# Where the partial sums of a seven-product block multiplication are combined, in a fp32 encoder trunk

## The chip, the core and the metric

The kernel runs on one core of one Trainium2 chip. The metric is the device time in microseconds (us) of one execution. TensorE (PE) multiplies matrices into PSUM, which has eight banks of 512 fp32 columns for each of the 128 partitions. ScalarE (ACT) and VectorE (DVE) read and write both PSUM and SBUF, GpSimd (POOL) here does small work and issues the transfers that add to what is in SBUF, and SyncE (SP) issues the plain loads.

## The reference

Two layers, each of them (`x` is 256 tokens by 1024):

```
x = x + 1/2 * SwiGLU_1(RMSNorm(x))      # w_gate, w_up: 1024 x 2816, w_down: 2816 x 1024
h = RMSNorm(x);  qA kA vA qB kB vB = h @ W_in
oA = windowed attention with a sink;  oB = differential attention
x = x + concat(oA, oB) @ W_out
x = x + 1/2 * SwiGLU_2(RMSNorm(x))      # silu(h @ w_gate) * (h @ w_up) @ w_down
```

and a last RMSNorm. All is fp32. There are four SwiGLU blocks (two in each layer); the change is in them.

## The kernel before

**Precision.** Each fp32 operand is split into a high part (a rounded copy, made by ACT, called a cast below) and a low part (the rest, made by a DVE subtraction). A product is then three matmuls: high by high, low by high, high by low. `emit_split` (line 191) splits weights in halves of a step: a step is a 512 x 512 weight block of 1 MB, half of it is 128 x 1024 elements, and its two parts take two of the 28 `s4` tiles.

**A SwiGLU block** (`ffn`, line 602) works through the 2816 columns in five groups of 512 and a rest of 256. A group makes gate and up products for both token halves (t = 0 and 1, 128 tokens each), silu, the product with the gate (`up`), the transposition of that hidden tile (`turn`), and the product with the down weights, whose sums for two halves of the 1024 outputs stay in four PSUM banks (`accs`) through the whole block.

**Seven products.** In a plain group the gate and up products are eight block products (token half by half of the 1024 inputs by gate/up) of 12 matmuls each. In the groups named in `SEVEN` (2, 3 and 4 in the first SwiGLU block, 1 to 4 in the other three, 15 groups in all) `by_seven` (line 637) makes seven, after Strassen and Winograd, out of sums of the operands. The sums on the token side come once per block from `make_sums`. On the weight side a group has the blocks a, b, c, d and uses a, b + c, d, c, a + b, a + b + c and a + b + c + d. Two of those additions are made by transfers that add (`gather`, issued by POOL: a gets b, b gets c), two by DVE (`plus`, line 131, in two instructions each). The seven products are then combined: ACT copies two of them out of PSUM (`m1`, `m7`), and DVE makes five further sums (`put`).

**What sets the order.** The instructions of PE, and here also of ACT, DVE and POOL, are kept in the order in which the program issues them (`Kept`, line 40; every instruction of theirs carries line 50). PE's order is written by hand. Around it, `weights(less, held)` (line 249) takes the next step for PE and first calls `ahead(2 * i + look[0] - less)`: this issues the splits of all half-steps up to that number, with the `prep` of a step (a `plus` or a `gather`) ahead of its splits, and the loads. When PE's third of four k-chunks of a step is issued, `part` calls `ahead` again for one half-step more, unless the step was taken with `held=True`. So `look[0]` is how many half-steps ACT and DVE are to be ahead of PE, and a split that is issued before another ACT or DVE instruction also runs before it. In the seven-product groups `look[0]` is 8, 7, 6, 5 for groups 1 to 4, and 6, 6, 5 for groups 2 to 4 of the first block.

**PSUM.** All PSUM tiles come from one pool of eight banks (`bank`, line 71). A tile gets a bank whose earlier tile has been read for the last time.

Of the kernel before, what the change touches and what calls it, by code (L numbers as in the profile page):

```python
# [9 lines left out]
F32 = mybir.dt.float32  # L10
F32R = mybir.dt.float32r
AF = mybir.ActivationFunctionType
ALU = mybir.AluOpType
# [21 lines left out]
def trunk(ctx: ExitStack, tc: tile.TileContext, x, n1, g1, u1, d1, nm, w_in, sink,  # L35
# [35 lines left out]
    def bank():  # L71
        return ps.tile([P, 512], F32, tag="ps", bufs=8, name=nm_("ps"))

# [18 lines left out]
    class Step:  # L92
        def __init__(self, kn, n, moves, key=None, prep=None, src=None, free=None, behind=None):
            self.kn, self.n, self.moves, self.prep = kn, n, moves, prep
            self.behind = behind
# [132 lines left out]
    def ahead(n):  # L228

        n = min(n, 2 * len(specs) - 1)  # L230
        while True:
            if at["split"] <= n and at["prep"] > at["split"] // 2:
# [26 lines left out]
    for l in range(DEPTH):  # L259
        def ffn_specs(wg, wu, wd, sevens):  # L260
# [3 lines left out]
            for g in range(1, NGRP):  # L264
                downs = [down(g - 1, h) for h in range(2)]
                if g in sevens:
                    specs.extend(seven(wg[l], wu[l], g * 512, downs, g == 1))
                else:
                    specs.extend(plain(w[l], g * 512, 512, k0, 4) for w in (wg, wu) for k0 in (0, 4))
                    specs.extend(downs)  # L270
            for k0 in (0, 4):
# [34 lines left out]
    class Norm:  # L306
# [42 lines left out]
        def make_sums(self):  # L349
# [18 lines left out]

            s1 = add(b1, t1, ALU.subtract)
            s2 = add(s1, t0, ALU.add)  # L370
            yield
            high(s1)
            high(s2)
            yield
            low(0, s1)
            b0_ = add(b0, s2, ALU.subtract)
            low(1, s2)
            v = add(t1, t0, ALU.subtract)
            yield
            high(b0_)  # L380
            high(v)
            yield
            low(2, b0_)
            low(3, v)
            yield
# [144 lines left out]
    def tokens(accs, xs, w, k0, ks=range(4), first=0, last=KC - 1, order=None, cols=slice(None), h=None):  # L530

        for k, t in (order or [(k, t) for k in ks for t in range(2)]):
            kk = k0 + k
            hi, lo = w.part(k, cols, h)
            xv = xs[kk // 2][:, kk % 2]
            xh, xl = xv[:, t * P:(t + 1) * P], xv[:, S + t * P:S + (t + 1) * P]
            pe.matmul(accs[t], lhsT=xh, rhs=hi, start=kk == first, stop=False)
# [22 lines left out]
    def first_groups(norm, ws):  # L560

        sls = [halves(bank()) for _ in ws]
        for k in range(0, KC, 2):
# [38 lines left out]
    def ffn(norm, aside=None, before=None, final=False, sevens=SEVEN[1]):  # L602
# [33 lines left out]

        def by_seven(h, g):


            flat = lambda: tmp().rearrange("p a n -> p (a n)")  # L640

            def put(o, x, y, op):
                dve.tensor_tensor(o, x, y, op=op)
                return o

            late, run = g == max(sevens), 1 in sevens
            m1, m7 = flat(), flat()


            if g > 1:  # L650
                g0 = prod(norm.quarter(0, 0), weights())
                act.copy(m1, g0)
                p7 = prod(norm.summed(3), weights(1, True))
                act.copy(m7, p7)
                hT = turn(h, 2)
                prod(norm.quarter(0, 1), weights(), g0)
                p3 = prod(norm.summed(2), weights())
                if not run:
                    g0 = silu(flat(), g0, 0)
                down(hT, g - 1, 0, weights())  # L660
                if run:
                    g0 = silu(flat(), g0, 0)
            else:
                p1 = prod(norm.quarter(0, 0), weights(1, True))
                hT = turn(h, (0,))
                w = weights(1, True)
                act.copy(m1, p1)
                p2 = prod(norm.quarter(0, 1), w)
                hT += turn(h, (1,))
                g0 = put(flat(), p2, m1, ALU.add)  # L670
                down(hT, 0, 0, weights())
                silu(g0, g0, 0)
                p3 = prod(norm.summed(2), weights())
                p7 = prod(norm.summed(3), weights(1, True))
                act.copy(m7, p7)
            h = blk(F32)
            p5 = prod(norm.summed(0), weights())
            prod(norm.summed(1), weights(look[0] - 5 if late else run, late or run), p7)
            u1 = put(m1, p7, m1, ALU.subtract)
            p4 = prod(norm.quarter(1, 1), weights(look[0] - 4 if late else 3 * run, late or run))  # L680
            g1 = put(flat(), p4, u1, ALU.subtract)
            w = weights(look[0] - 3 if late else 2 * run)
            silu(g1, g1, 1)
            put(u1, u1, p5, ALU.subtract)
            u0 = put(m7, u1, m7, ALU.subtract)
            put(u0, u0, p3, ALU.add)
            if run and g == max(sevens) - 1:
                ahead(2 * at["use"] - 2 + look[0] - 1)
            up(h, u0, g0, 0)
            up(h, u1, g1, 1)  # L690
            down(hT, g - 1, 1, w)
            return h

# [11 lines left out]

        accs = [[bank(), bank()] for _ in range(2)]

        def down(hT, g, h, w):
            tokens(accs[h], [None] * (2 * g) + hT, w, 4 * g, last=(FC - 1, G4 - 1) if final and h else FC - 1)


        gs, us = [bank(), bank()], [bank(), bank()]
        if before is None:
# [33 lines left out]
        for n in range(1, NGRP):  # L747
            if n in sevens:
                look[0] = IN_FFN + min(sevens) - n if before is not take_x else IN_MIX - (n == NGRP - 1)
                h = by_seven(h, n)  # L750
                continue
            sums = norm.make_sums()
            gs = [bank(), bank()]
            tokens(gs, norm.xs, weights(), 0)
            hT = turn(h, 2)
            norm.copies()
# [4 lines left out]
            us = [bank(), bank()]  # L761
# [4 lines left out]
            for hh in range(2):  # L766
                down(hT, n - 1, hh, weights())
                if hh == 0:
                    next(sums, None)

        gu = [bank(), bank()]
        tokens(gu, norm.xs, weights(), 0)
# [55 lines left out]
    def mix(l, norm, nxt_norm):  # L828
# [23 lines left out]

        def scores(q, kb, dist, slopes, init, den):

            sl = [bank(), bank()]
            for t in range(2):
# [19 lines left out]
        def soft_b(h, q):  # L876

            den = den_b[:, h]
            e, _ = scores(q, kbs["b", h], distB, [slopeB[h]] * 2, [3e38] * 4, den)
            d2 = den.rearrange("p (t a) -> p a t", a=2)  # L880
# [56 lines left out]
        vB = tp.tile([P, 2, 512], F32, tag="v", bufs=1, name=nm_("v"))  # L937
        vsl = [bank() for _ in range(2)]
        for k0 in (0, 4):
# [44 lines left out]
        oT = [blk() for _ in range(4)]  # L984
        rsl, osl = [[bank() for _ in range(2)] for _ in range(2)]
        for t in range(2):
# [175 lines left out]
```

## Time and profile before

| | us |
|---|---|
| time, median of 3 runs | 918.64 (917.53 to 919.39) |
| time of the profiled execution | 917.39 |
| its span, first to last instruction | 915.6 |
| TensorE busy (99% of the span) | 904.5 |
| VectorE busy (87%) | 792.5 |
| ScalarE busy (64%) | 589.8 |
| GpSimd busy (7%) | 66.4 |

A row of a timeline has the start, the length, the engine, the source line, the operation, the tile that is written and those that are read (w is a split weight, raw a loaded one, ps a PSUM tile, s an `s4` tile, q and v the token-side sums), and in brackets idle time before it with what ended that. Where several instructions are merged into one row, the length is that of all of them. Matmuls overlap: the time from one start to the next is what one costs PE.

### The profile page before, as it was taken

The page shows a single profiled execution, that of the slowest core. Times are in us where ns is not written, and L with a number is a line of the kernel's source. Part 1 is how long each engine was busy: PE and PEld are TensorE (multiplying, and loading weights), DVE is VectorE, ACT ScalarE, POOL GpSimd, SP SyncE. Part 2 cuts the span into 40 slices and gives each one's busy share as a digit, 9 for nine tenths or more (in the row PEclk, how much of TensorE's full clock was granted, in tenths as well). Part 3 has the DMA queues.
Part 4 walks back from the last instruction along what each step waited for, and adds up shares of the span by engine and source line. Part 5 has one row for each costly group of instructions (what it writes and reads, how often), then busy time and mean ns, then how long its engine had stood idle before and what let it go on. Part 6 is the DMA issues. An engine that isn't in the chain of part 4 may idle for free.

```text
span 915.6 us, 12544 instructions
## 1 busy us (share of the span) xinstructions
PE 904.5 (99%) x4696; PEld 763.7 (83%) x4696; DVE 792.5 (87%) x1096; ACT 589.8 (64%) x917; POOL 66.4 (7%) x83
## 2 busy tenths in 40 slices
PE   8999999999999999999999999999999999999997
PEld 6888888899888888888888888888998888888886
DVE  6768999959975999999789999997797689999994
ACT  7836676557865766576486666665677496666561
POOL 0400100000010100100010010000001010010011
PEclk9999999999999999999999999999999999999999
DMA  9996898828436698898767998887463467998831
GB/s 339 355 238 173 265 297 268 238 93 240 136 108 189 158 280 248 257 273 275 258 164 201 276 285 217 265 293 219 116 230 98 139 153 201 275 289 230 259 132 47
DMA packets 114061, 200.87 MB, mean 219 GB/s; under 512 B 3662, under 2 KB 31376, under 8 KB 114000
## 3 DMA queue, kind: packets, MB, share of 16 engines
q1 hardware_dynamic: 96528, 166.74, 54.5%
q0 software_dynamic: 16096, 31.75, 19.3%
q10 hardware_dynamic: 1376, 1.57, 0.5%
q8 instruction: 37, 0.61, 0.3%
q14 instruction: 24, 0.20, 0.1%
HBM read 199.00 MB, written 1.05 MB: 218 GB/s over the span
## 4 chain that ended last, share of the span: by engine, by line
PE 98%; issue 1%; DMA 0%; ACT 0%; DVE 0%; POOLq 0%; POOL 0%; ACTq 0%
PE ps L50 98%; DMA xk<-in_x_dram 0%; ACT w L50 0%; DVE s L50 0%; DVE xk L50 0%; ACT tmp L50 0%; ACT L50 0%; POOLq L1157 0%; POOL rf L50 0%; ACTq L50 0%; DVE tot L50 0%; DVE tmp L50 0%
## 5 line engine op out<-in xcount | busy, mean ns | idle before, releaser
L50 PE MATMUL ps<-w,s 128*128 128x512 f32 (+1 forms) x2574 | 600.2, 391 | 0.5 <-ACT tmp L50 0.5
L50 PEld LDWEIGHTS ps<-w,s 128*128 128x128 f32 x2574 | 477.6, 188 | 100.3 <-ACT tmp L50 2.3
L50 DVE TENSOR_TENSOR w<-raw,w 128x1024 fp32r<-128x1024 f32 (+1 forms) x458 | 482.1, 1101 | 37.8 <-ACT w L50 36.6
L50 ACT CAST w<-raw 128x1024 fp32r<-128x1024 f32 (+1 forms) x458 | 409.8, 954 | 122.6 <-DVE raw L50 78.4
L50 PE MATMUL ps<-w,q 128*128 128x512 f32 x540 | 127.3, 389 | 0.0
L50 PEld LDWEIGHTS ps<-w,q 128*128 128x128 f32 x540 | 101.4, 188 | 21.0
L50 PE MATMUL ps<-s,w 128*128 128x256 f32 x672 | 83.1, 284 | 0.0
L50 PEld LDWEIGHTS ps<-s,w 128*128 128x128 f32 x672 | 81.5, 192 | 0.5
L50 POOL DMA_DIRECT2D raw<-in_ffn_w_up_dram x30 | 38.9, 1296 | 472.8 <-DVE w L50 240.8
L50 DVE TENSOR_TENSOR raw<-raw,raw 128x1024 f32<-128x1024 f32 x60 | 70.7, 1219 | 0.0
L50 ACT ACTIVATE s<-ps,gcol 128x256 fp32r<-128x256 f32 (+1 forms) x80 | 31.7, 480 | 43.7 <-PE ps L50 42.1
L50 ACT CAST s<-ps 128x512 fp32r<-128x512 f32 x44 | 24.3, 594 | 29.9 <-PE ps L50 29.9
L50 PE MATMUL ps<-w,v 128*128 128x512 f32 x180 | 43.3, 389 | 0.0
L50 ACT COPY tmp<-ps 128x512 f32<-128x512 f32 x34 | 19.9, 585 | 36.2 <-PE ps L50 34.0
L50 ACT ACTIVATE s<-s,negm 128x256 f32<-128x256 f32 x64 | 31.9, 500 | 14.8 <-DVE negm L50 14.8
L50 PE MATMUL ps<-ident,s 128*128 128x128 f32 x304 | 39.7, 273 | 0.0
L50 PEld LDWEIGHTS ps<-w,v 128*128 128x128 f32 x180 | 33.8, 188 | 7.0
L50 PEld LDWEIGHTS ps<-ident,s 128*128 128x128 f32 x304 | 35.1, 140 | 5.1 <-issue 0.8
L50 DVE TENSOR_TENSOR s<-ps,s 128x512 fp32r<-128x512 f32 x44 | 28.7, 686 | 9.1 <-ACT s L50 9.1
L50 DVE SCALAR_TENSOR_TENSOR s<-ps,gcol,s 128x256 fp32r<-128x256 f32 x48 | 20.3, 478 | 11.6 <-ACT s L50 11.5
L50 DVE TENSOR_TENSOR tmp<-ps,tmp 128x512 f32<-128x512 f32 x37 | 25.4, 686 | 2.7 <-PE ps L50 2.1
L50 DVE TENSOR_TENSOR xk<-xk,ps 128x512 f32<-128x512 f32 (+1 forms) x25 | 14.1, 598 | 14.9 <-PE ps L50 14.9
(106 smaller groups left out, 404.7 us busy)
## 6 DMA issues: line engine op xcount, KB each, us to landing
raw<-in_ffn_w_down_dram SPq DMA_DIRECT2D x44, 1024.0 KB, 8.9
raw<-in_ffn_w_gate_dram SPq DMA_DIRECT2D x39, 1024.0 KB, 6.4
raw<-in_ffn_w_up_dram SPq DMA_DIRECT2D x39, 1024.0 KB, 5.7
raw<-in_ffn_w_up_dram POOLq DMA_DIRECT2D x30, 1024.0 KB, 12.3
raw<-in_w_in_dram SPq DMA_DIRECT2D x14, 1024.0 KB, 6.1
raw<-in_ffn_w_gate_dram SPq DMA_DIRECT2D x8, 512.0 KB, 6.2
raw<-in_ffn_w_up_dram SPq DMA_DIRECT2D x8, 512.0 KB, 7.2
raw<-in_w_in_dram SPq DMA_DIRECT2D x8, 512.0 KB, 5.3
```

The lines of the kernel that those rows point to most:

```text
L50: ins = issue(*a, **k)
```

## The change

The seven products of a group are combined mainly in PSUM. A new tile `xy` of two neighbouring banks is taken out of the pool (`pair`), which leaves six banks for everything else. ACT copies the first product, negated, into both banks of `xy`; two later products are added to those banks by PE, and another is copied by ACT into the bank of the first product, so that PE adds to it. DVE makes three sums instead of five. The token-side sums are combined with other signs. The weight sums are the same seven, taken in the order a, d, b + c, a + b, c, a + b + c, a + b + c + d: the product with c, which was the fourth, now lies between those with a + b and a + b + c. Both transfers that add stay. The DVE additions `plus` are one instruction of 128 x 2048 each instead of two of 128 x 1024, and that of c may be issued one step earlier (`early`).

The order changes too. The hidden tile is transposed one token half at a time (`turn_one`). The second down product of a group (`below`) moves into the next group, behind the first transposition; the first one lies between the third and the fifth product. The groups of a block run in one function, `by_sevens`. `lead` gives `look[0]`: 8, 8, 7, 7 for groups 1 to 4, and 6, 6, 5 for groups 2 to 4 of the first block. The splits of a + b + c + d are issued behind ACT's copy of the fifth product. Outside the seven-product groups some places that took two banks take `xy` instead, and `accs` is taken when it is first needed.

```diff
     def bank():
-        return ps.tile([P, 512], F32, tag="ps", bufs=8, name=nm_("ps"))
+        return ps.tile([P, 512], F32, tag="ps", bufs=6, name=nm_("ps"))
+
+    def pair():
+        return ps.tile([P, 2, 512], F32, tag="xy", bufs=1, name=nm_("xy"))
...
-    def seven(wg, wu, c0, downs, first):
+    def seven(wg, wu, c0, below, down):
...
         def plus(x, to):
             def prep():
-                for h in (0, 2):
-                    x_, t_ = [raws[i][:, h:h + 2] for i in (x, to)]
-                    dve.tensor_tensor(t_, t_, x_, op=ALU.add)
+                dve.tensor_tensor(raws[to], raws[to], raws[x], op=ALU.add)
             return prep
 
-        bc = Step(4, 512, load(b), key=b, behind=gather(c, b))
-        rest = [Step(4, 512, load(d), key=d, free=[]), Step(4, 512, load(c), key=c, free=[]), downs[0]]
-        steps = [rest[0], rest[2], rest[1], bc] if first else [bc] + rest
+        steps = [Step(4, 512, load(d), key=d, free=[]), Step(4, 512, load(b), key=b, behind=gather(c, b)), down]
+        if below is not None:
+            steps.insert(0, below)
         steps[0].prep = lambda: issue(gather(b, a), 1)
         return [Step(4, 512, load(a), key=a, free=[])] + steps + [
                 Step(4, 512, None, src=a, free=[]),
-                Step(4, 512, None, prep=plus(c, a), src=a, free=[c]),
-                Step(4, 512, None, prep=plus(d, a), src=a, free=[a, d]),
-                downs[1]]
+                Step(4, 512, load(c), key=c, free=[]),
+                Step(4, 512, None, prep=plus(c, a), src=a, free=[c], early=1),
+                Step(4, 512, None, prep=plus(d, a), src=a, free=[a, d])]
...
-                    (specs[at["prep"]].prep is None or at["split"] >= 2 * at["prep"]):
+                    (specs[at["prep"]].prep is None or at["split"] >= 2 * (at["prep"] - specs[at["prep"]].early)):
...
+        def turn_one(h, t):
+            sl = bank()
+            for k in range(4):
+                pe.transpose(sl[:, k * P:(k + 1) * P], h[:, t, k * P:(k + 1) * P], ident)
+            hb = blk()
+            act.copy(hb[:, 0], sl)
+            dve.tensor_tensor(hb[:, 1], sl, f(hb[:, 0]), op=ALU.subtract)
+            return hb
...
+            xy = pair()
+            for g in groups:
+                start, late = old is None, g == groups[-1]
+                look[0] = lead(g)
+                p1 = prod(norm.quarter(0, 0), weights(start, start))
+                act.activation(xy, p1.unsqueeze(1).to_broadcast([P, 2, 512]), AF.Copy, scale=-1.0)
+                if start:
+                    g0 = flat()
+                    act.copy(g0, p1)
+                new = [turn_one(h, 0)]
+                if start:
+                    p2 = prod(norm.quarter(0, 1), weights())
+                    new.append(turn_one(h, 1))
+                    dve.tensor_tensor(g0, p2, g0, op=ALU.add)
+                    prod(norm.summed(0), weights(), xy[:, 0])
+                    below(by_token(new), g - 1, 0, weights(max(look[0] - 7, 0), True), [(k, t) for t in range(2) for k in range(4)])
+                    silu(g0, g0, 0)
+                else:
+                    below(old, g - 2, 1, weights())
+                    new.append(turn_one(h, 1))
+                    prod(norm.quarter(0, 1), weights(), p1)
+                    prod(norm.summed(0), weights(), xy[:, 0])
+                    below(by_token(new), g - 1, 0, weights(max(look[0] - 7, 0), True))
+                    g0 = silu(flat(), p1, 0)
+                old = by_token(new)
+                p5 = prod(norm.summed(1), weights(look[0] - 5, True))
+                act.copy(p1, p5)
+                prod(norm.summed(2), weights(max(look[0] - 7, 0) if late else 0, late), xy[:, 1])
+                prod(norm.summed(3), weights(look[0] - 5 if late else 1, True), p5)
+                e = flat()
+                act.copy(e, p5)
+                u1, u0 = flat(), flat()
+                dve.tensor_tensor(u0, xy[:, 1], e, op=ALU.add)
+                dve.tensor_tensor(u1, xy[:, 0], e, op=ALU.add)
+                h = blk(F32)
+                up(h, u0, g0, 0)
+                p4 = prod(norm.quarter(1, 1), weights(look[0] - 4 if late else 3, True), p1)
+                g1 = flat()
+                dve.tensor_tensor(g1, p4, u1, op=ALU.subtract)
+                if late:
+                    w = weights(look[0] - 3)
+                else:
+                    ahead(2 * at["use"] + look[0] - 2)
+                silu(g1, g1, 1)
+                up(h, u1, g1, 1)
+            below(old, groups[-1] - 1, 1, w)
             return h
...
+        def lead(n):
+            return IN_FFN - (n - min(sevens)) // 2 if before is not take_x else IN_MIX - (n == NGRP - 1)
```

More of the change, by code (lines that the diff above doesn't have):

```diff
@@ L231, in ahead @@
         while True:
-            if at["split"] <= n and at["prep"] > at["split"] // 2:
+            if at["split"] <= n and at["prep"] > at["split"] // 2 and                     not (pending and specs[at["split"] // 2].added):
                 for _ in emit_split(*divmod(at["split"], 2)):
@@ L560, in first_groups @@
     def first_groups(norm, ws):
-        sls = [halves(bank()) for _ in ws]
+        both = pair()
+        sls = [halves(both[:, i]) for i in range(2)]
         for k in range(0, KC, 2):
@@ L635, in prod @@
             return acc
-        def by_seven(h, g):
-            flat = lambda: tmp().rearrange("p a n -> p (a n)")
[L642 to L691, printed above, removed]
@@ L760, in ffn @@
             next(sums, None)
-            us = [bank(), bank()]
+            us = both()
             for k0 in (0, 4):
@@ L765, in ffn @@
             h = hidden(g, us)
-            for hh in range(2):
+            for hh in range(1 if n + 1 == min(sevens) else 2):
                 down(hT, n - 1, hh, weights())
@@ L769, in ffn @@
                     next(sums, None)
-        gu = [bank(), bank()]
+        gu = both()
         tokens(gu, norm.xs, weights(), 0)
@@ L851, in q_finish, with scores @@
             return [q[:, 0], q[:, 1]]
-        def scores(q, kb, dist, slopes, init, den):
-            sl = [bank(), bank()]
+        def scores(q, kb, dist, slopes, init, den, wide=False):
+            both = pair() if wide else None
+            sl = [both[:, i] if wide else bank() for i in range(2)]
             for t in range(2):
@@ L937, in mix @@
         vB = tp.tile([P, 2, 512], F32, tag="v", bufs=1, name=nm_("v"))
-        vsl = [bank() for _ in range(2)]
+        both = pair()
+        vsl = [both[:, t] for t in range(2)]
         for k0 in (0, 4):
@@ L984, in mix @@
         oT = [blk() for _ in range(4)]
-        rsl, osl = [[bank() for _ in range(2)] for _ in range(2)]
+        rsl, both = [bank() for _ in range(2)], pair()
+        osl = [both[:, t] for t in range(2)]
         for t in range(2):
```

67 lines of the change are left out of this document (43 added, 24 removed).

## The prediction

> **What bounds the kernel now.** I read the page first, then the chain that ended last, then the waits, then the windows of three seven-product groups, and last their timeline.
>
> ```profile
> span 915.6 us, 12544 instructions
> ...
> PE 904.5 (99%) x4696; PEld 763.7 (83%) x4696; DVE 792.5 (87%) x1096; ACT 589.8 (64%) x917; POOL 66.4 (7%) x83
> ...
> PE 98%; issue 1%; DMA 0%; ACT 0%; DVE 0%; POOLq 0%; POOL 0%; ACTq 0%
> ```
>
> The chain in order of time says it more sharply: from 31 us to 905 us it never leaves PE.
>
> ```profile
> 31.04 873.94 PE ps L50 x4547
> ```
>
> The profiled execution took 917.39 us, 1.8 us more than its span, and the median of the runs is 918.64, 1.25 us above it. The waits that PE does have are small, and the windows of groups 2, 3 and 4 of the second SwiGLU block of layer 0 have none at all: 30.83 us busy of 30.83.
>
> ```profile
> PEld ps L50 <- ACT tmp L50: 2.3, 5, 0.9
> ...
> PEld ps L50 <- DVE w L50: 1.2, 4, 0.4
> ...
> PEld ps L50 <- ACT w L50: 0.7, 2, 0.4
> ...
> PE ps L50 <- ACT tmp L50: 0.5, 1, 0.5
> ```
>
> ```profile
> 338.14:368.97 30.83, 30.83 (x141) 25.61 (x140) 30.48 (x32) 20.95 (x25) 2.57 (x2) 1.00 0.92 262
> 368.97:399.80 30.83, 30.83 (x141) 25.61 (x140) 30.32 (x31) 20.18 (x24) 2.57 (x2) 1.00 0.94 263
> 399.80:430.60 30.80, 30.80 (x141) 25.59 (x140) 30.28 (x32) 19.37 (x24) 0.00 (x0) 1.00 0.88 267
> ```
>
> So PE is the bound, and DVE (third busy column, 30.3 to 30.5 us) is so close behind that whatever it has to do for PE at a given moment stands in a full queue. Two consequences: work taken from DVE or ACT gains nothing by itself, and any new place where PE waits for DVE costs its whole length.
>
> **What PE does after the change.** It still makes 84 matmuls of seven products and 48 of two down products per group, and eight transpositions. Their costs:
>
> ```profile
> 340.87 2.88 PE L50 MATMUL ps<-w,v 128*128 128x512 f32 x12
> 343.59 1.03 PE L50 MATMUL ps<-ident,s 128*128 128x128 f32 x8
> 344.38 3.01 PE L50 MATMUL ps<-w,s 128*128 128x512 f32 x12
> 347.23 2.88 PE L50 MATMUL ps<-w,q 128*128 128x512 f32 x12
> 349.95 5.60 PE L50 MATMUL ps<-w,s 128*128 128x512 f32 x24
> 355.39 5.60 PE L50 MATMUL ps<-w,q 128*128 128x512 f32 x24
> ```
>
> ```profile
> 309.98 0.60 PE L50 MATMUL ps<-ident,s 128*128 128x128 f32 x4
> 310.34 3.00 PE L50 MATMUL ps<-w,s 128*128 128x512 f32 x12
> 313.18 0.60 PE L50 MATMUL ps<-ident,s 128*128 128x128 f32 x4
> ```
>
> From start to start, a product is 2.72 us (347.23 to 349.95), a down product 5.44. Four transpositions cost 0.36 and make the next product 0.12 longer (310.34 to 313.18 is 2.84), eight cost 0.79 and 0.13: splitting them costs 0.04 us per group, nothing. PE's own work stays; what remains is whether it waits.
>
> **What DVE and ACT cost.** The groups by line in the same stretch, and the timeline for what an instruction costs in a queue:
>
> ```profile
> L50 DVE TENSOR_TENSOR w<-raw,w 128x1024 fp32r<-128x1024 f32 x34 | 39.9, 1222 | 0.4 <-ACT w L50 0.3
> ...
> L50 ACT CAST w<-raw 128x1024 fp32r<-128x1024 f32 x36 | 36.0, 1054 | 14.4 <-DVE raw L50 11.2 <-DMA raw<-in_ffn_w_up_dram 3.0
> ...
> L50 DVE TENSOR_TENSOR raw<-raw,raw 128x1024 f32<-128x1024 f32 x8 | 9.4, 1220 | 0.0
> ...
> L50 DVE TENSOR_TENSOR s<-ps,s 128x512 fp32r<-128x512 f32 x4 | 2.6, 686 | 0.0
> L50 ACT COPY tmp<-ps 128x512 f32<-128x512 f32 x4 | 2.4, 588 | 6.1 <-PE ps L50 6.1
> ```
>
> ```profile
> 339.92 1.42 DVE L50 SCALAR_TENSOR_TENSOR s<-tmp,hr,tmp 128x512 f32<-128x512 f32 x2
> ...
> 341.07 0.59 ACT L50 COPY tmp<-ps 128x512 f32<-128x512 f32 x1 [0.45 <-PE ps L50]
> 341.25 4.63 DVE L50 TENSOR_TENSOR w<-raw,w 128x1024 fp32r<-128x1024 f32 x4
> ...
> 343.79 0.59 ACT L50 COPY tmp<-ps 128x512 f32<-128x512 f32 x1 [2.13 <-PE ps L50]
> 344.27 1.08 ACT L50 CAST s<-ps 128x512 fp32r<-128x512 f32 x2
> ...
> 345.23 2.97 ACT L50 CAST w<-raw 128x1024 fp32r<-128x1024 f32 x3
> 345.79 1.29 DVE L50 TENSOR_TENSOR s<-ps,s 128x512 fp32r<-128x512 f32 x2
> ```
>
> In a queue a weight subtraction takes (4.63 - 1.22) / 3 = 1.14 us, a cast (2.97 - 1.05) / 2 = 0.96, a DVE sum with a PSUM operand 1.29 - 0.69 = 0.60, an `up` 0.67, an ACT copy out of PSUM 344.27 - 343.79 = 0.48; ACT sees a finished product 0.20 us after the next one begins (341.07 against 340.87). Per group two sums of about 0.7 go, 1.4 us of DVE's 30.4. The merged `plus` has no row; it lies between one subtraction's length, 1.22, and two, 2.44; I take 2.27, two places in the queue, as twice the elements come nearest to that. ACT's copy into both banks of `xy` has no row either: between one copy of 512 (0.48) and two casts of 1024 (1.92); I take 0.96, a cast of the same 1024 elements.
>
> The Trainium skill, page "ScalarE: Activation LUTs", section "Step-by-step: what each stage is for", says that ScalarE writes PSUM faster than SBUF, but that this helps only where TensorE does not need most of PSUM. [...]
>
> **The bank that is missing.** Six banks remain beside `xy`. From the second group of a block on, four hold the down sums and one holds the first product, which lives until the group's end. One is left, and both single transpositions and the fifth product need it in turn. So the second transposition must wait until ACT and DVE have read the first out. Before, four banks were left and both transpositions had their own. I walk the queues from t = 0, where PE begins the product with c, at a lead of 8.
>
> PE: c to 2.72, a + b + c to 5.44, a + b + c + d to 8.16, the next group's first product to 10.88, first transposition and its penalty 0.48, `below` 5.44: it wants to transpose again at 16.80.
>
> DVE: the subtractions of a + b + c + d are held behind the copy of the fifth product. That copy starts at 0.20, the first cast 0.48 later, its subtraction 1.05 after that: 1.73. Behind it stand six subtractions (half-steps up to 2 x 6 + 1 + 8): 8.57. Then two sums and one `up`: 10.44; the last sum: 11.04; three subtractions issued by the extra `ahead`: 14.46; the other `up`: 15.13; three more from the next `weights`: 18.55. Only now comes the low half of the first transposed tile, done at 19.24. PE waits 2.4 us.
>
> At a lead of 7 there is one subtraction less in front: 18.10, a wait of 1.3. From group 2 to 3 the lead changes and the sum is also 1.3 (part of it at the first transposition, whose bank is freed by the last sum). In group 1 banks are free, but a down product waits: after the first product (2.72 + 0.20) ACT has the copy into `xy`, a copy and the high half (0.96 + 0.48 + 0.48), then casts; DVE starts at 5.89 with three subtractions, a `plus` and one more: 12.72, and the second tile's low half is done at 13.41. PE reaches the matmul that needs it at 2.72 + 0.36 + 2.84 + 0.36 + 2.84 + 2.72 + 0.23 = 12.07: 1.3 us. A block of four groups: 1.3 + 2.4 + 1.3 + 1.3 = 6.3; three such blocks 18.9. The first block, with leads of 6, 6, 5, has four subtractions in the first burst and the last sum tied to PE: the low half is done at 17.16, 0.4 us late once.
>
> **The gathers.** Both stay. The load of b moves up one half-group and its gather, behind the free slot of c, starts about when PE begins c; the gather of b into a starts when the next a is split, at 6.6. The two are now in flight together.
>
> ```profile
> raw<-in_ffn_w_up_dram POOLq DMA_DIRECT2D x30, 1024.0 KB, 12.3
> ```
>
> ```profile
> ACT w L50 <- DMA raw<-in_ffn_w_up_dram: 40.3, 20, 10.6
> ```
>
> The cast of b + c is the third of the second burst and stands ahead of a silu, whose `up` DVE reaches at 14.46. Cast and silu take 1.66, so a landing at 12.4 is just in time: at the median the gather costs nothing, and each us beyond it costs 1 us at up to 12 group changes. ACT waits already (40.3 us in 20 places). I take 0.3 us on average, 4 us; the ends are 0 and 2 us each, 24.
>
> **The rest.** The mixing stage uses eight banks either way; `xy` is taken for score, value and output tiles whose readers finish before the next user. I cost it at nothing; the cover is the product or transposition between two users, and if one were late it would be about a sum, 0.7 us, per layer. `plus` as one piece lets a cast start 1.1 us later; PE uses those weights two products later, so nothing.
>
> **Sum.** 917.39 + 18.9 + 0.4 + 4 = 940.7 against the profiled execution; against the median, 1.25 more, 941.9. I say 941.
>
> **Rivals.**
>
> *No new wait.* DVE loses 1.4 us per group; if it then runs ahead far enough that the burst is shorter than I walk, the bank is free in time. For it: not one wait in three groups before. Against it: the burst is set by the order of issue, not by DVE's load. Time: 918 to 920.
>
> *Faster.* One mechanism: the lighter DVE queue delivers weights earlier where PE waits for ACT and DVE now, 2.3 + 1.2 + 0.7 + 0.5 = 4.7 us at most: 914. It decides if none of the walk's waits is over 0.3 us. Against it: those waits lie outside the groups whose queue gets lighter.
>
> *Gathers first.* If both in flight land 2 us later than the median, 24 us instead of 4: 961. For it: DMA is at 0.88 to 0.94 of its time in these windows.
>
> The bank wait has a page of its own: the Trainium skill, "Perfetto Trace Analysis", section "Optimizing Tensor Performance", has independent groups rotate through different banks so that reading one out overlaps the next; two transpositions on one bank break that. No row of before can show it, as there PE has no such gap; by the page alone each of them would wait for the read-out, which is what I walked.
>
> **Chances.** The bank wait as walked 0.77, gathers first 0.15, no new wait 0.05, faster 0.03. A change under 0.2%, 1.8 us, can't be told from none. The range leaves out the two small cases and the far end of the gathers: from 926 (half of each wait, the gathers at nothing: 918.64 + 9.6 = 928, less 2 for the estimates) to 955 (1.4 us of late gather at each change).
>
> **What would show it.** After: PE idle in front of transposition matmuls, about 11 or 12 times, 1 to 2.5 us each, released by DVE writing s; in group 1 a gap in front of a down product; DVE's share below 0.85, with the same matmul count. Wrong: these gaps missing, or PE waiting for w after a wait of ACT on the up weights, or waits in the mixing stage.

## The result, and the profile after

The kernel after the change takes 947.33 us in the median (944.61 to 948.38, 4 runs), against 918.15 of the kernel before in the same comparison (917.53 to 919.39): a ratio of 1.0312, interval 1.0287 to 1.0336. The profiled execution took 944.61 us against 917.39: 27.2 us more.

The page of the kernel after; its lines answer to the three of before:

```profile
span 942.8 us, 12414 instructions
...
PE 911.4 (97%) x4696; PEld 764.9 (81%) x4696; DVE 768.5 (82%) x1036; ACT 601.6 (64%) x935; POOL 65.5 (7%) x83
...
PE 62%; DVE 17%; DMA 10%; ACT 6%; issue 4%; POOLq 0%; ACTq 0%; POOL 0%; DVEq 0%
...
L50 DVE TENSOR_TENSOR raw<-raw,raw 128x2048 f32<-128x2048 f32 x30 | 68.6, 2287 | 0.5
```

The matmuls are as many as before, and DVE has 24 us less to do. But the chain that ended last, 98% PE before, now runs over DVE and over transfers for a quarter of the span. The waits of the kernel after say where PE stands (us in total, times, the longest; PEld is TensorE's load of a weight, in front of its matmul):

```profile
DVE w L50 <- ACT w L50: 74.4, 57, 4.1
...
ACT w L50 <- DMA raw<-in_ffn_w_up_dram: 61.4, 23, 6.6
...
PEld ps L50 <- DVE s L50: 24.3, 14, 2.9
...
PE ps L50 <- DVE s L50: 18.4, 14, 2.4
...
PEld ps L50 <- DVE tmp L50: 1.8, 3, 0.6
```

The third and fourth lines are the same 14 places, at which TensorE waits for a tile that DVE writes; before there was one such place, of 0.2 us. The windows of groups 2, 3 and 4 of the second block, which were full before, now have 2.35, 0.99 and 1.20 us without PE work, and the first of them a clock of 0.95 (span of the window, busy time of PE, PEld, DVE, ACT and POOL, granted clock, DMA share, GB/s):

```profile
336.17:371.20 35.03, 32.68 (x141) 26.61 (x140) 29.50 (x28) 21.56 (x26) 2.57 (x2) 0.95 0.90 249
371.20:403.50 32.30, 31.31 (x141) 25.41 (x140) 29.49 (x29) 21.61 (x26) 2.57 (x2) 1.00 0.85 249
403.50:435.81 32.31, 31.11 (x142) 25.49 (x140) 28.63 (x28) 20.89 (x24) 0.00 (x0) 1.00 0.88 256
```

And the change of group from which the prediction's walk was made, in the timeline of the kernel after. (The fifth product is `p5` in the kernel, the one with a + b; its copy is the row at 328.27.)

```profile
327.71 1.28 POOL L50 DMA_DIRECT2D raw<-in_ffn_w_up_dram  x1 [23.82 <-DMA raw<-in_ffn_w_up_dram]
...
328.01 2.88 PE L50 MATMUL xy<-w,q 128*128 128x512 f32 x12
328.27 0.57 ACT L50 COPY ps<-ps 128x512 f32<-128x512 f32 x1 [4.32 <-PE ps L50]
328.75 5.80 ACT L50 CAST w<-raw 128x1024 fp32r<-128x1024 f32 x6
329.83 6.90 DVE L50 TENSOR_TENSOR w<-raw,w 128x1024 fp32r<-128x1024 f32 x6 [2.05 <-ACT w L50]
...
336.65 1.28 DVE L50 TENSOR_TENSOR tmp<-xy,tmp 128x512 f32<-128x512 f32 x2
...
338.51 0.68 DVE L50 TENSOR_TENSOR tmp<-ps,tmp 128x512 f32<-128x512 f32 x1
...
339.11 3.48 DVE L50 TENSOR_TENSOR w<-raw,w 128x1024 fp32r<-128x1024 f32 x3
...
340.18 1.05 ACT L50 CAST w<-raw 128x1024 fp32r<-128x1024 f32 x1 [3.25 <-DMA raw<-in_ffn_w_up_dram]
...
342.51 0.74 DVE L50 SCALAR_TENSOR_TENSOR s<-tmp,hr,tmp 128x512 f32<-128x512 f32 x1
343.18 3.49 DVE L50 TENSOR_TENSOR w<-raw,w 128x1024 fp32r<-128x1024 f32 x3
...
346.58 0.68 DVE L50 TENSOR_TENSOR s<-ps,s 128x512 fp32r<-128x512 f32 x1
...
347.32 0.66 PE L50 MATMUL ps<-ident,s 128*128 128x128 f32 x4 [2.35 <-DVE s L50]
```

With t = 0 at 328.01, the two sums begin at 8.64 (walked 8.57), the low half of the transposed tile at 18.57 (18.55), and PE stands still for 2.35 us (2.4). The same rows hold a second thing: the transfer that adds c to b, issued at 327.71, lands for the cast at 340.18. That cast ends at 341.23, and DVE takes its result as the third of the three subtractions from 339.11, at 339.11 + 2 x 1.14 = 341.39. The transfer is in time by 0.16 us. The experiments turn on this.

### The profile page after: what moved, and what is told of

Read it like the earlier page. It is cut to its first block, busy times and chain, and to the rows that moved or that the text cites. A ratio compares the mean times of both kernels' runs of the same rounds, so it can differ in the third digit from the quotient of the medians.

```text
span 942.8 us, 12414 instructions
## 1 busy us (share of the span) xinstructions
PE 911.4 (97%) x4696; PEld 764.9 (81%) x4696; DVE 768.5 (82%) x1036; ACT 601.6 (64%) x935; POOL 65.5 (7%) x83
## 4 chain that ended last, share of the span: by engine, by line
PE 62%; DVE 17%; DMA 10%; ACT 6%; issue 4%; POOLq 0%; ACTq 0%; POOL 0%; DVEq 0%
PE ps L50 45%; PE xy L50 18%; DVE w L50 11%; DMA raw<-in_ffn_w_up_dram 10%; DVE s L50 3%; ACT w L50 2%; ACT s L50 2%; DVE raw L50 2%; DVE tmp L50 1%; DMA xk<-in_x_dram 1%; ACT xy L50 0%; ACT ps L50 0%; DVE q L50 0%; ACT tmp L50 0%; DVE rc L50 0%
## 5 line engine op out<-in xcount | busy, mean ns | idle before, releaser
L50 PE MATMUL ps<-w,s 128*128 128x512 f32 (+1 forms) x2046 | 485.9, 393 | 3.5 <-DVE s L50 3.5
L50 PEld LDWEIGHTS ps<-w,s 128*128 128x128 f32 x2046 | 381.4, 190 | 82.7 <-DVE s L50 4.7
L50 PE MATMUL xy<-w,s 128*128 128x512 f32 x528 | 125.2, 391 | 0.0
L50 PEld LDWEIGHTS xy<-w,s 128*128 128x128 f32 x528 | 98.4, 188 | 20.3
L50 PE MATMUL xy<-w,q 128*128 128x512 f32 x360 | 86.9, 390 | 0.0
L50 PEld LDWEIGHTS xy<-w,q 128*128 128x128 f32 x360 | 67.4, 188 | 14.0
L50 DVE TENSOR_TENSOR raw<-raw,raw 128x2048 f32<-128x2048 f32 x30 | 68.6, 2287 | 0.5
L50 PE MATMUL ps<-s,w 128*128 128x256 f32 x480 | 59.3, 284 | 0.0
L50 PEld LDWEIGHTS ps<-ident,s 128*128 128x128 f32 x304 | 34.7, 140 | 27.3 <-DVE s L50 19.6
L50 DVE TENSOR_TENSOR s<-ps,s 128x512 fp32r<-128x512 f32 x44 | 29.7, 683 | 17.1 <-ACT s L50 17.1
L50 PE MATMUL ps<-w,q 128*128 128x512 f32 x180 | 43.2, 389 | 0.0
L50 PEld LDWEIGHTS ps<-w,q 128*128 128x128 f32 x180 | 33.8, 188 | 7.0
```

The costliest lines, as they stand in the source:

```text
L50: ins = issue(*a, **k)
```

## The experiments

All of them are edits of the kernel after, except e8, which is one of the kernel before. Up to four kernels were timed together, each batch with the kernel before, whose medians were 919.14 (e1 to e4), 917.62 (e5 to e8), 918.60 (e9 to e11) and 918.15 (e12). "Waits" is worked out from each trace: the start-to-start time of two matmuls, less the 0.227 us that 512 columns take (0.110 for a transposition), summed where it is over 0.215 us, between 33 and 925 us. A trace is of one execution, whose time can differ from the median (944.61 for the kernel after, 951.79 for e3_lead8). "Half clock" is the number of stretches of 3.41 us at a granted clock of 0.5 in there, and what the matmuls in them lost beside the waits.

| kernel | median us | ratio to before, interval | waits us | half clock |
|---|---|---|---|---|
| before | 918.15 | 1 | 0.0 | 0 |
| after | 947.33 | 1.0312 (1.0287 to 1.0336) | 22.7 | 2, 3.2 us |
| e1_hold | 943.01 | 1.0263 (1.0245 to 1.0282) | 22.3 | 0 |
| e2_lead6 | 945.60 | 1.0298 (1.0271 to 1.0324) | 22.2 | 3, 4.0 us |
| e3_lead8 | 957.42 | 1.0405 (1.0374 to 1.0437) | 30.7 | 2, 2.4 us |
| e4_nogather | 942.14 | 1.0247 (1.0230 to 1.0264) | 21.6 | 2, 2.6 us |
| e5_banks | 942.65 | 1.0264 (1.0242 to 1.0286) | 22.4 | 1, 1.3 us |
| e6_nohold | 951.45 | 1.0366 (1.0345 to 1.0386) | 26.8 | 3, 4.5 us |
| e7_hold_lead7 | 941.30 | 1.0255 (1.0236 to 1.0274) | 17.5 | 2, 3.2 us |
| e8_before_seven | 932.85 | 1.0166 (1.0146 to 1.0185) | 14.5 | 3, 3.2 us |
| e9_burst | 954.72 | 1.0389 (1.0374 to 1.0405) | 29.7 | 5, 6.6 us |
| e10_outside | 943.89 | 1.0276 (1.0261 to 1.0292) | 20.8 | 1, 1.6 us |
| e11_banks_lead7 | 942.23 | 1.0267 (1.0247 to 1.0288) | 20.5 | 0 |
| e12_both | 925.85 | 1.0083 (1.0060 to 1.0107) | 7.6 | 0 |

The theory at the start is the prediction's: six banks force the second transposition to wait for the read-out of the first, and that read-out stands behind a burst of subtractions whose length the lead sets. Its rivals: the gathers, and a DVE or ACT that is late in any case.

**Length of the burst.** A lead of 8 in all groups of blocks 2 to 4 puts one more subtraction in front of the tile at two of the three changes of a block:

```diff
-            return IN_FFN - (n - min(sevens)) // 2 if before is not take_x else IN_MIX - (n == NGRP - 1)
+            return 8 if before is not take_x else IN_MIX - (n == NGRP - 1)
```

> The lead is 8 in all groups of blocks 2 to 4. Bank theory: the second and third change of group become like the first, 0.3 and 2.2 us each, so 9.1 us a block instead of 6.5: about 8 us more, and up to nine waits long enough for the clock to drop at 1.6 us each instead of two to four: 953 to 963. Gathers as the cause: the same time or a little less, 942 to 948.

It came out as walked: 2.61, 0.35 + 2.42 and 0.35 + 2.54 us in the second block, and 957.42 in the median. The other way, a lead of 6 (the same line with a 6):

> The lead is 6 in all groups of blocks 2 to 4. Bank theory: two subtractions fewer stand in the queue than at 8, so the waits shrink, by the same walk to 1.4, 0.4 and 0.4 us and none in group 1: 2.2 us a block instead of 6.5, and no drop of the clock: 944.6 - 3 x 4.3 - 3.1 = 929 us. Gathers as the cause: less lead leaves them less time, 950 or more.

Both expectations missed, with 945.60. The wait in group 1 went, and at the first change of group the wait shrank to 1.30 us in blocks 2 and 3, where the walk said 1.4. But the later ones, walked at 0.4, grew (2.04 and 1.53 in the second block, 2.60 and 4.03 in the third). At the longest of them ACT stands 4.44 us for a transfer onto `raw`, until 593.26, with the copy into `xy` and the high half of the transposed tile queued behind that cast, and DVE stands 2.02 us for the cast. A shorter lead shortens the burst, and the transfers become what is late.

**Order in the queue.** The first product's step is taken with less and without the further half-step, so that the tile's low half stands ahead of the second three subtractions:

```diff
-                p1 = prod(norm.quarter(0, 0), weights(start, start))
+                p1 = prod(norm.quarter(0, 0), weights(1 if start else 2, True))
```

> Bank theory (the second transposition waits until DVE has made the low half of the first transposed tile, which stands behind three subtractions of the next weights): these are now issued behind it, so the waits of about 2.5, 1.0 and 1.4 us per block in front of the second transposition go, and with the 2.5 us waits the drops of the clock; the wait of 1.3 us at the down product of group 1 and 0.35 us at the first transposition from group 2 to 3 stay. 944.6 - 3 x 4.9 - 3.1 = 927 us. Rivals (the second half of the hidden tile comes late from its up instruction; or late gathers hold ACT): nothing that they depend on moves, 944 to 948.

> The first product of a group takes its weights with one or two half-steps less and without the further half-step, as in e1, and the lead is 7 in all four groups. If the length of VectorE's queue ahead of the transposed tiles is what counts, both edits shorten it by one subtraction each: by the walk of the queues a block waits 1.5 us instead of 6.2 (0.5 in group 1, 0.2 and 0.8 at a first transposition), and no wait is long enough for a half-clock stretch: 927 to 931. If VectorE is short of time as such (e1 had as many us of waits as the change, at other places), the waits come back elsewhere: 939 to 943.

e7 adds a lead of 7 in all groups to it. Waits of e1:

```profile
ACT w L50 <- DMA raw<-in_ffn_w_up_dram: 67.8, 24, 6.1
...
PEld ps L50 <- DVE s L50: 14.3, 13, 1.6
...
PEld ps L50 <- DVE tmp L50: 8.8, 6, 1.6
```

e1 came to 943.01, a little under what its rivals said and 16 us above the bank theory. The waits at the second transposition are gone, as the edit meant, but the sum of the waits is hardly less, 22.3 against 22.7: PE now waits at a first transposition for the last sum (1.1 to 1.3 us, the third line) and at the down product for the second tile. Only the long waits went, and with them the half clock. e7 has the lowest median of the rearrangements, 941.30, though its interval overlaps that of e1; the walk said 927 to 931, and the rival, a VectorE that is short of time as such, 939 to 943. At this point the prediction's cause was in doubt.

**The gathers alone.** The transfer that adds c to b is left out (the product with b + c uses b):

```diff
-        steps = [Step(4, 512, load(d), key=d, free=[]), Step(4, 512, load(b), key=b, behind=gather(c, b)), down]
+        steps = [Step(4, 512, load(d), key=d, free=[]), Step(4, 512, load(b), key=b), down]
```

> Leaves out the addition of c to b (one transfer less per group; other values). Bank theory: only what the waits have beyond the walk goes, 0.4 to 1.0 us in the fourth block and 0.4 in the first: 942 to 946. Gathers as the cause: most of the 27 us goes, 920 to 928.

Its waits, and its chain from the page:

```profile
ACT w L50 <- DMA raw<-in_ffn_w_up_dram: 2.3, 2, 1.6
```

```profile
PE 68%; DVE 19%; ACT 5%; issue 5%; DMA 3%; SPq 0%; DVEq 0%; POOLq 0%; POOL 0%; ACTq 0%
```

ACT hardly waits for transfers any more, the chain has lost most of its DMA (3% against 10%) and kept DVE, and PE waits at the same places for 21.6 us. The gathers by themselves are not what costs 27 us.

**The banks alone.** In blocks 1 to 3 both down sums share two banks until the rest of the columns, which gives the pool two more (the sums of the second half are mixed into the first):

```diff
...
-                accs.append([bank(), bank()])
+                accs.append(accs[0] if accs and not final else [bank(), bank()])
...
```

> Two more free banks: in the first three SwiGLU blocks both halves of the down product are summed into the same two banks until the rest of 256 columns (so the sums of the second half are left out of the output and mixed into the first); the fourth block is as in the changed kernel. Same matmuls, same order, same casts and subtractions. Bank theory (the prediction's): the waits at the second transposition (2.5 and 2.6, 1.0, 1.4 us) and the 0.35 us at the first go in blocks 1 to 3, 5.2 us in each of blocks 2 and 3 and 0.8 in block 1, about 11 us, and one or two half-clock stretches of 1.6 us with them: 933 to 935 against 947; the 1.3 us in group 1 stays, and block 4 keeps all of its waits as a control. Rival (VectorE's queue is late by itself, and the bank is only the first thing that shows it): the waits move to the next matmuls that need that queue or ScalarE's, the first transposition or the product that is added to the first one; less than half of them goes: 940 to 945.

942.65 is on the rival's side, and this decided against the prediction's cause. In the second block the waits were 1.31, 2.51, 0.35 + 0.96 and 1.36 (6.5 us). In e5 they are 1.31, 0.49, 0.65, 0.85, 0.24, 0.83, 0.89 and 0.60 (5.9 us), and in the third block 7.0 against 6.6. In the first block two waits for weights, 0.44 and 0.70 us, stand in place of 0.37 and 0.77. The timeline of e5 shows what stands in the place of the bank:

```profile
346.02 3.02 PE L50 MATMUL ps<-w,s 128*128 128x512 f32 x12 [0.33 <-ACT xy L50]
...
353.15 3.02 PE L50 MATMUL ps<-w,s 128*128 128x512 f32 x12 [0.49 <-DVE s L50]
```

The second transposition no longer waits, and the product behind it waits for ACT's copy into `xy`, then the down product for the second tile. The bank is the place where PE first meets the queue, not the reason why the queue is late. The median is 4.7 us lower all the same; the profile has one half-clock stretch where the kernel after has two, and its single waits are shorter. e11 puts e5 and e7 together:

> e5 and e7 together: two more free banks in blocks 1 to 3 (down sums of the second half mixed into the first, so the output is not the reference's), the first product's step held, and a lead of 7 in all groups of blocks 2 to 4. If bank and queue length are both needed to make PE wait, the waits of e7 at a first transposition (1.1 us, for a bank) go and nothing takes their place: 930 to 934. If the queues of VectorE and ScalarE are late in any case, the waits move on to the transposition's own input and the down product: 937 to 941.

942.23 is 1.2 us more than the second theory gave, but the waits moved on, as it says; their sum is 20.5 us, against 17.5 in e7.

**The hold.** The casts of the last weight sum are no longer held behind the copy of the fifth product:

```diff
-                p5 = prod(norm.summed(1), weights(look[0] - 5, True))
+                p5 = prod(norm.summed(1), weights(0, True))
```

> The splits of the last weight sum are no longer held behind the copy of the fifth product: the step of the fifth product is taken without the five half-steps less. If the hold is the cause (VectorE idles 2.0 to 3.1 us per group in front of the held burst, while ScalarE waits 4.7 us for that product), the burst starts about 2 us earlier and each wait at a second transposition shrinks by up to 2 us, to 0.5, 0 and 0 in a block: 10 us of waits and the half-clock stretches go: 931 to 935. Rival (the order in the queue counts, not when it starts): the copy now stands behind five casts, PE waits 0.5 to 1.4 us for the fifth product's bank in most groups, and the transposition waits stay: 943 to 949.

951.45, on the rival's side and 2.5 us beyond it. Waits and timeline of e6:

```profile
PEld ps L50 <- ACT ps L50: 15.5, 11, 2.7
```

```profile
327.90 2.95 ACT L50 CAST w<-raw 128x1024 fp32r<-128x1024 f32 x3 [3.87 <-DVE raw L50]
330.75 0.59 ACT L50 COPY ps<-ps 128x512 f32<-128x512 f32 x1
...
331.39 2.81 PE L50 MATMUL ps<-w,v 128*128 128x512 f32 x11 [0.42 <-ACT ps L50]
```

The copy now stands behind three casts, and PE waits for the bank of the fifth product, because the product with a + b + c, the next but one, is added there. The change has made that copy part of PE's path, and the hold is its price.

**Work in the burst and outside of it.** e9 leaves out DVE's subtractions for a + b + c + d, which begin the burst, e10 those for a + b + c, which DVE makes ahead of it. The high part is used for the low part, which then takes no `s4` tile. The edit of e9:

```diff
...
-            dve.tensor_tensor(l_, r_, f(h_), op=ALU.subtract)
+            if s.skip:
+                loaded[i].parts[-1] = (hi, hi)
+            else:
+                dve.tensor_tensor(l_, r_, f(h_), op=ALU.subtract)
...
-                Step(4, 512, None, prep=plus(d, a), src=a, free=[a, d])]
+                Step(4, 512, None, prep=plus(d, a), src=a, free=[a, d], skip=True)]
```

> Leaves out VectorE's two subtractions for a + b + c + d in each of the 15 seven-product groups; its high part is used in place of its low part, so the output is not the reference's. Casts, matmuls and orders stay. These two subtractions, 2.3 us, are the first of the burst behind the copy of the fifth product, on the chain fifth product, copy, burst, low half of the first transposed tile, second transposition. If that chain is the cause, each wait at a transposition is up to 2.3 us shorter: 2.5 to 0.3, 0.35 + 1.0 and 1.4 to nothing; the 1.3 us in group 1 stays; no half-clock stretch: 926 to 930. If VectorE's work as a whole is the cause: also 34 us less work, 930 to 938, and e10 the same. If ScalarE's queue holds the transposed tile back: 943 to 948.

> The control to e9: leaves out as many subtractions, those for a + b + c (its high part is used for its low part; output not the reference's), which VectorE makes ahead of the copy of the fifth product, where it then idles 2.0 to 3.1 us in front of the held burst. Chain theory: VectorE idles longer there and nothing else moves, waits as in the changed kernel: 944 to 948. VectorE's work as a whole: as e9, 930 to 938.

e10 came to 943.89 and kept the waits of the second block within 0.02 us (2.52, 0.35 + 0.97, 1.36). DVE idles 4.43 us in front of the burst, where it idled 2.05:

```profile
331.23 6.91 DVE L50 TENSOR_TENSOR w<-raw,w 128x1024 fp32r<-128x1024 f32 x6 [4.43 <-ACT w L50]
```

So it is not the sum of DVE's work. In e10 the nine transfers of c into b at the changes of group of blocks 2 to 4 also landed earlier, which the edit did not aim at: after 8.7 us on average, against 11.3 in the kernel after. The waits beyond the walk in block 4 went (0.96 and 1.36 us are left there), the others stayed. With the burst as long as before, an early landing gains no more than in e4. e9 went to 954.72, which no theory had said. Its timeline, where the product with c begins at 331.49:

```profile
331.74 0.57 ACT L50 COPY ps<-ps 128x512 f32<-128x512 f32 x1 [4.30 <-PE ps L50]
332.22 5.79 ACT L50 CAST w<-raw 128x1024 fp32r<-128x1024 f32 x6
...
335.20 4.63 DVE L50 TENSOR_TENSOR w<-raw,w 128x1024 fp32r<-128x1024 f32 x4 [3.93 <-ACT w L50]
339.75 1.28 DVE L50 TENSOR_TENSOR tmp<-xy,tmp 128x512 f32<-128x512 f32 x2
...
344.17 1.05 ACT L50 CAST w<-raw 128x1024 fp32r<-128x1024 f32 x1 [3.78 <-DMA raw<-in_ffn_w_up_dram]
...
345.25 1.23 DVE L50 TENSOR_TENSOR w<-raw,w 128x1024 fp32r<-128x1024 f32 x1 [0.69 <-ACT w L50]
...
350.47 0.69 DVE L50 TENSOR_TENSOR s<-ps,s 128x512 fp32r<-128x512 f32 x1
```

Two things took the 2.3 us back. ACT still makes six casts in 5.79 us, and DVE can't run ahead of them: the sums begin at 8.26 instead of 8.64. Then DVE stands 0.69 us for the cast that waits for c in b, which begins at 344.17 (12.68 after the product with c; 12.17 in the kernel after). The low half comes at 18.98 instead of 18.57. The same nine transfers took 12.1 us on average in e9; why they take longer here and less in e10 stays open.

**Both chains.** That gave a new theory: two chains of nearly equal length end at the low half, the burst (copy, casts, subtractions) and the landing of c in b, and each hides the other. e12 shortens both: it leaves out the casts and subtractions of a + b + c + d (its product takes the parts of a + b + c), and the transfer:

```diff
...
+        if s.skip:
+            loaded[i].parts.append(loaded[i - 1].parts[j])
+            if j == 1:
+                for k in s.free:
+                    raws.pop(k)
+            return
...
-        steps = [Step(4, 512, load(d), key=d, free=[]), Step(4, 512, load(b), key=b, behind=gather(c, b)), down]
+        steps = [Step(4, 512, load(d), key=d, free=[]), Step(4, 512, load(b), key=b), down]
...
-                Step(4, 512, None, prep=plus(d, a), src=a, free=[a, d])]
+                Step(4, 512, None, prep=plus(d, a), src=a, free=[a, d], skip=True)]
```

> Leaves out two things at once: both the casts and the subtractions of a + b + c + d (its product takes the parts of a + b + c instead), and the transfer that adds c to b (as in e4); the output is not the reference's. Theory of two chains of equal length: the transposed tile's low half waits for the later of the burst (copy of the fifth product, casts at 0.97 us on ScalarE, subtractions) and the landing of c in b, 12.4 us after the product with c begins, and each alone hides behind the other (e4 and e9 gained nothing by taking one away). With both shorter the sums and the low half come about 2 us earlier: waits of 2.5, 0.35 + 1.0 and 1.4 us in a block become 0.5, 0 and 0, the 1.3 us of group 1 stays, no half-clock stretch: 923 to 929. If neither burst nor landing is the cause, as e9 taken alone would say: 940 to 946.

925.85, inside what the theory said. Page, waits and, with the product with c beginning at 326.76, DVE's two rows of e12:

```profile
PE 907.0 (98%) x4696; PEld 763.3 (83%) x4696; DVE 734.9 (80%) x1006; ACT 573.4 (62%) x905; POOL 46.2 (5%) x68
...
PE 82%; DVE 11%; ACT 4%; issue 2%; DMA 0%; POOLq 0%; POOL 0%; ACTq 0%; DVEq 0%
```

```profile
PEld ps L50 <- DVE s L50: 9.3, 10, 1.6
...
ACT w L50 <- DMA raw<-in_ffn_w_up_dram: 0.6, 1, 0.6
```

```profile
333.13 1.28 DVE L50 TENSOR_TENSOR tmp<-xy,tmp 128x512 f32<-128x512 f32 x2
...
343.20 0.69 DVE L50 TENSOR_TENSOR s<-ps,s 128x512 fp32r<-128x512 f32 x1
```

The sums begin at 6.37 instead of 8.64, the low half at 16.44 instead of 18.57. Of 22.7 us of waits 7.6 are left: three times 1.3 in group 1, which come ahead of both chains, 0.4 at the first change of group of each block and 0.4 at the last of blocks 2 to 4, and twice 0.5 in the mixing stage. The banks are still six. One case is missing: casts and subtractions left out with the transfer kept. That the transfer alone would then hold the tile is argued, from e9's rows and from the 0.16 us of margin above, and not shown.

**A faster kernel.** No rearrangement of the change came near the kernel before. e8 tried that one with seven products in all 16 groups:

```diff
-SEVEN = ((2, 3, 4), (1, 2, 3, 4))
+SEVEN = ((1, 2, 3, 4), (1, 2, 3, 4))
```

> The kernel before the change with seven products in group 1 of the first block too, so that all 16 groups have them. 12 matmuls less, 2.72 us of PE. If PE does not wait more: 2.5 us less than before, 916.2. If the token-side sums, which must then be made in the first group of the first block while ScalarE and VectorE still prepare the block's operands, come late: 1 to 3 us of new waits there, 917 to 920.

Twelve matmuls less, and 932.85: more than either expectation said. The timeline of e8:

```profile
38.29 0.47 PE L50 MATMUL ps<-ident,s 128*128 128x128 f32 x1 [4.31 <-DVE s L50]
...
57.38 0.78 PE L50 MATMUL ps<-w,v 128*128 128x512 f32 x2 [4.04 <-ACT w L50]
```

In the first block neither the hidden tile nor the summed weights are there in time: PE waits 4.5 us before 38.29 and 4.2 before 57.38, and the granted clock there is 0.5 for 6.83 and 3.41 us.

## Why the prediction was right, point by point

- **The walk of the queues.** Walked for blocks 2 to 4: 18.9 us. Measured: 6.5 + 6.6 + 7.5 = 20.6, of which 1.0 in block 4 goes when the transfer of c is left out (1.33 and 1.96 against 0.98 and 1.36 in e4). That leaves 19.6. One by one: 2.4 walked and 2.5 to 2.6 measured, 1.3 and 0.35 + 0.96, 1.3 and 1.36, and in group 1 1.3 and 1.31. The places are those named, the gap in front of the down product included. The first block: 0.4 walked, 0.37 + 0.77 measured, and 0.39 in e4, without the transfer of c.
- **Its cause.** Here a step failed, though the number held. "So the second transposition must wait" for a bank is true of the kernel, but two more banks took next to nothing off the sum of the waits (22.4 against 22.7 us in e5; in e11 it is 20.5, more than the 17.5 of e7). Behind the bank stand the tile's own parts, in a queue whose order the change fixed: the copy of the fifth product has to precede six casts (e6), and these the sums. The prediction walked that queue rightly and took its last link for its cause; the number held because the read-out that frees the bank is the row at which that queue ends.
- **The gathers.** 4 us were put in; by the trace of e4 they cost 1.0 us in block 4 and 0.75 in block 1. The median of e4 is 5.2 us lower; its mean clock of 0.995 to 0.996, against 0.992 to 0.994, would explain more of that, but no trace shows which stretches went. That the transfer is "just in time" was right: 0.16 us of margin in the rows above. What was not seen is that it forms a second chain beside the burst, so that neither can be shortened alone.
- **What was left out.** The half clock: 3.2 us in the profile. The mixing stage was put at nothing with 0.7 us per layer if its cover failed; it waits 0.47 us once per layer, for ACT. That was one of its signs of being wrong. The other signs came as said: 11 waits at transpositions for DVE (2 in the first block, 0.96 to 2.60 us in the other three), the gap in front of the down product, DVE at 82% and as many matmuls.
- **The durations without a row.** The merged `plus` takes 2.29 us (2.27 taken). The copy into `xy` takes 1.0 us (0.96 taken). ACT's copies of 512 columns out of PSUM take 570 ns into PSUM and 585 into SBUF. The Trainium skill's sentence on this ("ScalarE: Activation LUTs", section "Step-by-step: what each stage is for"), that ScalarE writes PSUM faster than SBUF, agrees with these copies by 15 ns, too little to show in this sum.
- **The sum.** In the profiled execution 19.6 + 0.4 + 1.7 + 0.9 + 3.2 = 25.8 of the 27.2 us (the walked waits, first block, gathers, mixing, half clock); of the rest about 0.8 is in waits shorter than 0.215 us and 0.6 behind the start of the last matmul. The forecast for this execution, 940.7, had 2.3 us too much for the gathers and nothing for the half clock and the mixing stage, 4.1; that these cancel in part is luck. The median of the runs is 2.7 us above that execution, at a mean clock of 0.992 to 0.993 against 0.994 there; more half-clock stretches would explain it, but no trace of those runs shows it.

## What to carry to other kernels

When a product is combined by the engine that is the bound, each copy that it now needs from another engine is a new edge in its path, and the order around that copy (here a hold) delays everything queued behind it; the work taken from VectorE, 24 us, bought nothing against that here. Where a wait is found, free its resource by itself before calling it the cause: the bank was the place, and freeing it moved the wait on. And when shortening either of two suspects gains next to nothing, shorten both in one run, since chains of equal length hide each other.

## What the runs showed of the hardware that was not expected

A PE wait of 2 to 3 us can cost more than itself. In the kernel after, 0.6 us behind the wait that ends at 347.32, the granted clock is 0.5 for 3.41 us, in a window with full PE work. The same twelve matmuls take 4.58 us behind that wait and 2.99 behind an equally long one that ends at 813.69:

```profile
347.91:351.32 3.41, 3.41 (x10) 2.63 (x9) 1.62 (x2) 2.70 (x4) 0.00 (x0) 0.50 1.05 406
```

```profile
347.73 4.58 PE L50 MATMUL ps<-w,s 128*128 128x512 f32 x12
...
814.10 2.99 PE L50 MATMUL ps<-w,s 128*128 128x512 f32 x12
```

That is 1.6 us on top of 2.5. In all traces together 38 waits were 2.0 us or longer; such a stretch came with 21 of them (the shortest 2.04, in e2) and not with the other 17 (2.52 in e10, 2.70 in e3, 2.81 in e9). In e7 it twice followed a pair of short waits close together (0.84 and 1.15 us, 0.87 and 1.15); a pair of 1.34 and 1.15 in e11 had none. Each lasted 3.41 us, but for one of 6.83, twice that, in e8 (the low clock at the very end, where PE has no more work, is left out). The Trainium skill, page "TensorE: Matmul & The Clock Gate", section "What's actually happening", gives a free-running window of 3413 ns, which agrees with that length. In its section "Why this matters for your kernels" the same page of the Trainium skill asks for no idle gaps over about 3 us; here 2.0 us was enough at times. In its section "A second HAM failure mode: psum-queue depth-cycling" the Trainium skill tells of short idle times between groups of matmuls, frequent enough that the clock goes down and up again; the pairs in e7 are the nearest to that here.
